# Stick keys' first eight k-tiles as a ninth seven-product group, woven with the sparse gate's first chunk, and the first taps issued before the values

## The chip, the cores and the metric

One core of a Trainium2 chip runs the whole kernel. The metric is the device time of one execution in microseconds; lower is better. Five engines work side by side, each through its own list of instructions: PE (TensorE, matmuls into PSUM), DVE (VectorE), ACT (ScalarE), POOL (GpSimd, which here issues DMAs) and SP (SyncE, which issues DMAs).

## What is computed

The reference is a decoder trunk of two layers over 256 tokens of 2048 features, in float32. Each layer projects its normalised input with one wide matrix and feeds three token mixers. Cut to what the change touches:

```python
h = rms_norm(x, norm_w)
proj = h @ w_in
(qa, ka, va, za, qi, ki, wi, ub, zb, qc, kc, vc, zc, gates) = jnp.split(proj, split_points(), axis=-1)
y_a = (dsa_attention(qa, ka, va, qi, ki, wi, top_k) * jax.nn.silu(za)) @ w_a_out
y_b = (conformer_conv(ub, conv_w, conv_b, cln_w, cln_b) * jax.nn.silu(zb)) @ w_b_out
kc = kc.reshape(b, s, C_HEADS, HEAD_DIM)
y_c = (stick_breaking_attention(qc, kc, vc) * jax.nn.silu(zc)) @ w_c_out
x = x + merged @ w_out
```

`kc` (1024 columns) are the keys of the stick-breaking attention, "stick keys" below. `za` (1024 columns) is the gate of the sparse attention. `conformer_conv` holds a causal depthwise convolution of 31 taps over 1024 channels.

## The kernel before, in words

**Units.** Weights arrive in units of two k-tiles by 512 columns (512 KB), by SP's queue into one of five `raw` buffers (`load_unit` L228, `raw_unit` L418). Float32 accuracy comes from splitting: ACT rounds the unit into `wh` (`high`, L255), DVE subtracts that from it into `wl` (`low`, L259), and PE forms three of the four products of high and low parts (`mult`, L270): 12 matmuls of 128x512 for 256 tokens. `wh` and `wl` have three buffers each, so the rounding of a unit waits until PE is through with the unit three before it. A chunk is 512 output columns: eight units, summed in two PSUM banks (`acc`, four banks in all; `mm` tiles, two of two banks each, serve for the rest).

**Leaving the banks.** `chunk_F` (L331) ends in `turned` (L308): DVE transposes the two banks into `zt` (L299, one buffer), POOL writes `zt` to DRAM (L302) and reads it back as `zy` (L308), and ACT or DVE then use it. The banks are free after DVE's transposes.

**Seven-product groups.** Class `Seven` (L459) does the first eight k-tiles of two chunks at once by a Strassen-like scheme: 14 half units of six matmuls in place of eight units of 12. The price is sums of weights on DVE (L511, L512, L524: 128x1024 each), some sums made by the DMA itself (`accum_op`, issued by POOL at L517 and L528), and a copy and a difference of banks (L573, L579). A group holds four `acc` banks (X, Y, Z, W). Eight such groups run per layer. The weights that are read twice lie in `ar` and in `ph` and `pl`. `gather` and `run` interleave a group's half units with plain units ("weave"), whose banks are then a two-bank `mm` tile (`wide_accs`).

**The taps.** The convolution is summed in one tile (`cv`) by `taps`: a tap is four `tap` instructions on DVE (L731, 128x256 each), or four products on ACT (L726) into a spare tile and one addition on DVE (L1032, 128x1024). `drain` (L205), called behind a unit's subtraction, issues the next piece; `pace` says of which kind ("2": two DVE taps, "s": products into `one`, of which there is one buffer, and their addition at the next call), `hold` stops it. A product group into `one` can start only when the addition of the group before it has read `one`.

**Order of a layer.** `values(0)`, `index_chunk(0)` and `index_chunk(4)` (each eight units, which share a bank of low-part products: ten matmul times per unit rather than 12), the convolution's input group `u` woven with the indexer's key steps, two more index chunks, the sparse keys and queries, the stick queries (two chunks), the stick keys (two chunks), the sparse gate (two chunks), `values(1)`, and so on. The sparse attention's three jobs (`attend`, L1297) run in the background of the stick queries, the stick keys and the gate; each of them goes through POOL's round trip once, and its last matmuls (L1355) wait for that. The scheduler keeps each engine's instructions in the order in which they were written, but for some that are marked as high in priority.

Of the kernel before, what the change touches and what calls it, by code (L numbers as in the profile page):

```python
# [14 lines left out]
P = 128  # L15
S = 256
NT = S // P
D = 2048
KD = D // P
CW = 1024  # L20
KC = CW // P
DEPTH = 2
NH = 8
# [7 lines left out]
LATER = 10  # L31
# [8 lines left out]
O_QA, O_KA, O_VA, O_ZA = 0, 1024, 1280, 1536  # L40
O_QI, O_KI, O_WI = 2560, 4608, 4736
O_UA, O_UG, O_ZB = 4752, 5776, 6800
O_QC, O_KC, O_VC, O_ZC, O_G = 7824, 8848, 9872, 10896, 11920
# [8 lines left out]
def trunk(ctx: ExitStack, tc: tile.TileContext, x, w_in, xt, w_a, w_b, w_c, w_out,  # L52
# [51 lines left out]
    def slot(dt=F32):  # L104
        return sp.tile([P, KC, S], dt, tag="s8", bufs=13, name=nm("s8"))
# [7 lines left out]
    def parts(n):  # L113
        return [slot(F32R).rearrange("p (k w) t -> p k w t", w=2) for _ in range(n // 4)]

    class Lazy(list):
        def __init__(self, n, make):
            super().__init__([None] * n)
            self.make = make
# [33 lines left out]
    waiting = []  # L153
# [11 lines left out]
    @contextmanager  # L165
    def in_turn():
        with tc.high_priority(offset=URGENT), issue_after(newest_parts[1].ins):
            yield
# [34 lines left out]
    hold, calls, pace, urgent = [False], [0], ["2"], [False]  # L203
# [106 lines left out]
    def turned(srcs, use, later=LATER, tmp=None, soon=False):  # L310


        n = len(srcs)
        if tmp is None:
            tmp = tp.tile([P, n * 512], F32, tag="zt", bufs=1, name=nm("zt"))
        c = srcs[0].shape[1]
        z = away([v.rearrange("p (k e) -> p k e", e=P) for v in srcs], tmp[:, :n * c], soon)

        def rest():
            y = tp.tile([P, n * 512], F32, tag="zy", bufs=1, name=nm("zy"))  # L320
            y = y[:, :n * c].rearrange("p (u k i) -> p u k i", u=n * 4, i=32)
            back(z, y)
            yield later - 2
            yield from use(y)

        pending.append([count[0] + 2, rest()])
# [7 lines left out]
    def chunk_F(w, c0, act, nk, use, later=LATER):  # L334
        turned(chunk_N(w, [(c0, 512)], act, nk), use, later)
# [81 lines left out]
    ring, spare = [0], [0]  # L417
# [24 lines left out]
    def once(make):  # L442
        kept = []

        def get():
            if not kept:
                kept.append(make())
            return kept[0]

        return get  # L450
# [8 lines left out]
    class Seven:  # L459


        def __init__(self, w, cols, act, sums, lead=7, own=None, adds=False):
            self.banks = banks = {}
            self.steps = {}

# [8 lines left out]
                return source(w, k * 4 + h * 2, 2, cols[n])  # L474

            area = [ar[:, h * 1024:(h + 1) * 1024].rearrange("p (k c) -> p k c", k=2) for h in range(2)]
            homes = area if own is None else {}
            third = {}

            def after_raw():  # L480
                return issue_after(last_raw[0].ins) if last_raw[0] is not None else nullcontext()

            def two(h):
                if own is not None:
                    homes[h] = own()[:, h * 1024:(h + 1) * 1024].rearrange("p (k c) -> p k c", k=2)
                with after_raw():
                    nc.sync.dma_start(homes[h], block(0, 1, h))

            def three(h):
                g = ("ph", "pl")[h]  # L490
                if own is not None:
                    third[h] = area[h]
                else:
                    third[h] = tp.tile([P, 1024], F32, tag=g, bufs=1, name=nm(g)).rearrange("p (k c) -> p k c", k=2)
                with after_raw():
                    nc.sync.dma_start(third[h], block(1, 1, h))
# [219 lines left out]
    def gate(c0, o, b, w, hx, done=None, attended=None):  # L716
        for k in range(0, KC, 4):
            chunk_F(w, c0 + k * P, hx, KD, partial(gate_use, k, o, b, (lambda k=k: done.count(k // 4) < NT) if done is not None else None, alone=done is attended),
                    LATER + 2 if k else LATER - 1)
# [47 lines left out]
    for layer in range(DEPTH):  # L767
# [255 lines left out]
        def taps(j, yT=yT, cv=cv, pr=pr, one=one, two=two, halves=halves):  # L1023

            o = cv[:, j * 4:j * 4 + 4, :]
            o2 = o.rearrange("p (t c) f -> p t (c f)", t=NT)
            state = dict(q=1, c=0, sum=None)

            def added():
                if state["sum"] is None:  # L1030
                    return False
                nc.vector.tensor_add(o2, o2, state["sum"])  # L1032
                state["sum"] = None
                return True

            halves.append(added)

            def begin():
                products_of(yT, pr, j, 0, o2, True)

            def go():
                by = pace[0][calls[0]]
                if added() and by == "s":
                    by = ""
                q = state["q"]
                if q < TAPS and by:
                    if state["c"] or by == "2":
                        for c in range(2):
                            tap(yT, cv, pr, j * 4 + state["c"] + c, q)
                        state["c"] = (state["c"] + 2) % 4  # L1050
                    else:
                        state["sum"] = one if by == "s" else two[:, q % 2]
                        products_of(yT, pr, j, q, state["sum"])
                    state["q"] += not state["c"]
                if state["q"] < TAPS or state["sum"] is not None:
                    waiting.insert(0, [0, [go]])

            waiting.append([4, [begin]])
            waiting.append([1, [go]])

        def use_u(j, y, yT=yT):
# [111 lines left out]
        def index_chunk(h):  # L1173
            acc, low_ = token_accs(), low_tile()
            for k0 in range(0, KD, 2):
                if (h, k0) in between:
                    between[h, k0]()
                background(index_unit(acc, low_, k0, unit(w, k0, 2, [(O_QI + h * P, 512)])))
            index_done(h, acc, low_)
# [8 lines left out]
        def values(j):  # L1188
            a = chunk_N(w, [(O_VC + j * 512, 512)], hx, KD, accs=None if j else wide_accs())
            if j:  # L1190
                with in_turn():
                    for f in halves:
                        f()
            for t in range(NT):
                with tc.high_priority():
                    nc.scalar.copy(vcr[:, t, j * 512:(j + 1) * 512], a[t])

        values(0)
        index_chunk(0)
        index_chunk(4)  # L1200
        def turn_first():
            with in_turn():
                turned(sgs, partial(use_u, 0))

        keys = key_steps()
        keys[7].at(0, turn_first)
        ring[0], spare[0] = 0, 10 ** 9
        run(gather("y*2 g.M1a y g.M5a g.M1b y g.M5b y g.M6a y g.M6b y g.M2a y g.M2b g.M7a g.M7b g.M3a c g.M3b c g.M4a d g.M4b c d c d d",
                   g=u, y=keys, c=ug, d=ua))
# [152 lines left out]
        for job in ((1, (0,)), (0, (0, 1)), (1, (1,))):  # L1362
            start(attend(*job))
        chunk_F(w, O_QC + 4 * P, hx, KD, partial(use_q, 4))
        pace[0] = "s2"

        kcT = slot()

# [1 line left out]
            nc.scalar.copy(blocks(kcT[:, h:h + 4, :]), by_feature(y))  # L1370
            yield 0

        for h in range(0, NH, 4):
            chunk_F(w, O_KC + h * P, hx, KD, partial(use_k, h))
        pace[0] = "s2"
        ga = parts(KC)
        gate(O_ZA, qaT, ga, w, hx, attended, attended)
        values(1)
        finish()
        settle()  # L1380
# [481 lines left out]
```

## Time and profile before

| what | value |
|---|---|
| median of 3 runs | 1982.86 us (1982.69 to 1982.94) |
| the profiled execution | 1982.91 us |
| its span in the trace | 1981.1 us |
| PE busy | 1970.6 us, 99% of the span |
| DVE busy | 1724.0 us, 87% |
| ACT busy | 1302.1 us, 66% |
| granted clock of TensorE | 0.999 of full speed |

PE is busy nearly all the time; its matmuls are pipelined, so a busy time says that matmuls followed each other, not how fast. The two layers have the same stages; the second runs some 983 us after the first. Times below are from the span's start.

### The profile page before, as it was taken

Reading aid. Unit: us, or ns where it says so; the run is one execution under the profiler, and the core shown is the slowest. Engines: PE = TensorE matmul, PEld = TensorE weight load, DVE = VectorE, ACT = ScalarE, POOL = GpSimd, SP = SyncE. Lnnn points to the kernel's source line nnn. Section 1 sums busy time; section 2 is a strip of 40 time slices with the busy share of each in tenths; the row PEclk is TensorE's granted clock in tenths of the full one; section 3 lists DMA queues with packets and bytes.
Section 4 is the critical chain, followed back from the end, with each engine's and each line's share of the span. In section 5 each row is a group of like instructions: output and inputs, shape, how many; then the busy total and the mean of one; then the engine's idle time right before and its main releaser. Section 6 shows DMA issues by size and latency. Waiting matters only on the chain. (4 is left out here: it accounts for less than half of the span.)

```text
span 1981.1 us, 26165 instructions
## 1 busy us (share of the span) xinstructions
PE 1970.6 (99%) x9194; PEld 1648.1 (83%) x9194; DVE 1724.0 (87%) x2054; ACT 1302.1 (66%) x1668; POOL 215.0 (11%) x320
## 2 busy tenths in 40 slices
PE   9999999999999999999999999999999999999998
PEld 8888888888888888888888888888888888888886
DVE  8798999989988979878786989999888888798786
ACT  7567666579875666564565666565898766565654
POOL 0021111200200001011100210121001000010010
PEclk9999999999999999999999999999999999999999
DMA  8888768876878778787978887688669688787894
GB/s 277 278 262 261 239 180 262 257 223 188 260 239 264 212 228 271 243 273 271 321 232 277 252 264 224 192 259 273 200 188 279 213 276 250 217 276 235 288 287 137
DMA packets 247557, 486.90 MB, mean 246 GB/s; under 512 B 17984, under 2 KB 30784, under 8 KB 247296
## 3 DMA queue, kind: packets, MB, share of 16 engines
q1 hardware_dynamic: 217472, 406.03, 63.2%
q0 software_dynamic: 28288, 76.04, 14.6%
q10 hardware_dynamic: 1664, 3.15, 0.4%
q8 instruction: 72, 1.18, 0.2%
q14 instruction: 61, 0.50, 0.1%
HBM read 452.38 MB, written 32.77 MB: 245 GB/s over the span
## 5 line engine op out<-in xcount | busy, mean ns | idle before, releaser
L270 PE MATMUL acc<-wh,s 128*128 128x512 f32 x4096 | 1039.8, 390 | 0.0
L255 ACT CAST wh<-raw 128x1024 fp32r<-128x1024 f32 (+1 forms) x639 | 666.9, 1046 | 416.6 <-PE acc L270 271.2
L259 DVE TENSOR_TENSOR wl<-raw,wh 128x1024 fp32r<-128x1024 f32 (+1 forms) x640 | 773.3, 1213 | 154.7 <-ACT wh L255 147.0
L270 PEld LDWEIGHTS acc<-wh,s 128*128 128x128 f32 x4096 | 761.4, 188 | 153.2 <-DVE acc L579 0.5
L270 PE MATMUL acc<-wl,s 128*128 128x512 f32 x1856 | 517.0, 390 | 0.0
L270 PEld LDWEIGHTS acc<-wl,s 128*128 128x128 f32 x1856 | 346.0, 188 | 74.8 <-DVE wl L259 4.4
L270 PE MATMUL mm<-wh,s 128*128 128x512 f32 (+1 forms) x1376 | 335.2, 385 | 0.0
L270 PEld LDWEIGHTS mm<-wh,s 128*128 128x128 f32 x1376 | 257.3, 188 | 50.9 <-ACT ev L1688 0.5
L302 POOL DMA_DIRECT2D z<-zt x192 | 113.2, 612 | 795.6 <-DVE zt L299 743.4
L270 PE MATMUL mm<-wl,s 128*128 128x512 f32 (+1 forms) x688 | 180.9, 385 | 0.0
L255 ACT CAST wh<-ar 128x1024 fp32r<-128x1024 f32 x92 | 96.9, 1053 | 81.0 <-PE acc L270 33.6
L270 PEld LDWEIGHTS mm<-wl,s 128*128 128x128 f32 x688 | 128.7, 188 | 24.4
L259 DVE TENSOR_TENSOR wl<-ar,wh 128x1024 fp32r<-128x1024 f32 x92 | 112.1, 1220 | 21.1 <-ACT wh L255 21.1
L731 DVE SCALAR_TENSOR_TENSOR s<-yT,cst,s 128x256 f32<-128x256 f32 x216 | 94.5, 476 | 0.1
L726 ACT ACTIVATE ar<-yT,cst 128x256 f32<-128x256 f32 x192 | 83.7, 499 | 15.4 <-DVE t L1330 12.6
L255 ACT CAST wh<-va 128x1024 fp32r<-128x1024 f32 x55 | 57.7, 1050 | 44.8 <-PE acc L270 19.5
L259 DVE TENSOR_TENSOR wl<-va,wh 128x1024 fp32r<-128x1024 f32 x55 | 67.1, 1219 | 20.6 <-ACT wh L255 20.6
L528 POOL DMA_DIRECT2D ar<-in_w_in_dram x28 | 33.8, 1220 | 453.0 <-DVE wl L259 453.0
L270 PEld LDWEIGHTS mm<-s,wl 128*128 128x128 f32 x512 | 66.9, 191 | 5.0
L308 POOL DMA_DIRECT2D zy<-z x50 | 36.1, 722 | 293.2 <-DMA z<-zt 75.8
L270 PE MATMUL mm<-s,wl 128*128 128x192 f32 x512 | 66.0, 271 | 0.0
L726 ACT ACTIVATE s<-yT,cst 128x256 f32<-128x256 f32 x88 | 40.4, 517 | 38.3 <-DVE s L1032 38.1
(284 smaller groups left out, 1463.3 us busy)
## 6 DMA issues: line engine op xcount, KB each, us to landing
raw<-in_w_in_dram SPq DMA_DIRECT2D x500, 512.0 KB, 4.6
raw<-in_w_out_dram SPq DMA_DIRECT2D x50, 512.0 KB, 5.5
zy<-z POOLq DMA_DIRECT2D x48, 512.0 KB, 5.8
z<-zt POOLq DMA_DIRECT2D x184, 128.0 KB, 5.0
ar<-in_w_in_dram SPq DMA_DIRECT2D x28, 512.0 KB, 6.3
ar<-in_w_in_dram POOLq DMA_DIRECT2D x28, 512.0 KB, 9.6
raw<-in_w_b_dram SPq DMA_DIRECT2D x26, 512.0 KB, 5.1
raw<-in_w_a_dram SPq DMA_DIRECT2D x24, 512.0 KB, 6.2
```

Source lines behind the costliest of these rows:

```text
L255: newest_parts[0] = nc.scalar.copy(u[1], u[0])
L259: newest_parts[1] = sub = nc.vector.tensor_sub(u[2], u[0], u[1].bitcast(F32))
L270: newest[0] = nc.tensor.matmul(o, lhsT, rhs, start=start, stop=stop, skip_group_check=True)
L302: nc.gpsimd.dma_start(z[:, :, :, a, :].rearrange("t b c e -> c (t b) e"), tmp[a * 32:(a + 1) * 32].rearrange("c t b k i -> c (t b) (k i)"))
L308: nc.gpsimd.dma_start(y.rearrange("p (t a) k i -> p t (a k i)", a=4), z.rearrange("t b c a e -> (b c) t (a e)"))
L528: nc.gpsimd.dma_start((homes if own is None else third)[h], block(1, 0, h), accum_op=ALU.add)
L726: nc.scalar.activation(v, yT[:, c, q:q + S], AF.Identity if bias else AF.Copy, scale=wq, **b)
L731: nc.vector.scalar_tensor_tensor(o, yT[:, c, q:q + S], wq, o, op0=ALU.mult, op1=ALU.add)
```

## The change

The change has three parts.

1. `Seven` takes `room`, two makers of slots in which the twice-read weights lie, in place of `ar`, `ph` and `pl`.
2. The stick keys' first eight k-tiles become such a group (`kg`). Its 14 half units are woven with the eight plain units of the gate's first chunk, which sum in a two-bank `mm` tile; the keys' last eight k-tiles (4 and 4 plain units, `kc_` and `kd_`) follow in the four `acc` banks; then comes the gate's second chunk as before. The keys' two chunks are turned at their last units with delays of 8 and 10 units.
3. The turn that gives the first half of the convolution's input stands ahead of `values(0)`, and the taps may run during `values(0)` and the two index chunks, at pace "s"; afterwards they are held until `u` as before. Pace "s2" around the stick queries and keys becomes "s".

```diff
--- before.py
+++ after.py
@@ -459,7 +459,7 @@
     class Seven:
 
 
-        def __init__(self, w, cols, act, sums, lead=7, own=None, adds=False):
+        def __init__(self, w, cols, act, sums, lead=7, own=None, adds=False, room=None):
             self.banks = banks = {}
             self.steps = {}
 
@@ -474,21 +474,23 @@
                 return source(w, k * 4 + h * 2, 2, cols[n])
 
             area = [ar[:, h * 1024:(h + 1) * 1024].rearrange("p (k c) -> p k c", k=2) for h in range(2)]
-            homes = area if own is None else {}
+            homes = area if own is None and room is None else {}
             third = {}
 
             def after_raw():
                 return issue_after(last_raw[0].ins) if last_raw[0] is not None else nullcontext()
 
             def two(h):
-                if own is not None:
-                    homes[h] = own()[:, h * 1024:(h + 1) * 1024].rearrange("p (k c) -> p k c", k=2)
+                if own is not None or room is not None:
+                    homes[h] = (own() if room is None else room[0]())[:, h * 1024:(h + 1) * 1024].rearrange("p (k c) -> p k c", k=2)
                 with after_raw():
                     nc.sync.dma_start(homes[h], block(0, 1, h))
 
             def three(h):
                 g = ("ph", "pl")[h]
-                if own is not None:
+                if room is not None:
+                    third[h] = room[1]()[:, h * 1024:(h + 1) * 1024].rearrange("p (k c) -> p k c", k=2)
+                elif own is not None:
                     third[h] = area[h]
                 else:
                     third[h] = tp.tile([P, 1024], F32, tag=g, bufs=1, name=nm(g)).rearrange("p (k c) -> p k c", k=2)
@@ -1055,7 +1057,7 @@
                 if state["q"] < TAPS or state["sum"] is not None:
                     waiting.insert(0, [0, [go]])
 
-            waiting.append([4, [begin]])
+            waiting.append([4 if j else 0, [begin]])
             waiting.append([1, [go]])
 
         def use_u(j, y, yT=yT):
@@ -1195,15 +1197,13 @@
                 with tc.high_priority():
                     nc.scalar.copy(vcr[:, t, j * 512:(j + 1) * 512], a[t])
 
+        turned(sgs, partial(use_u, 0), LATER - 2)
         values(0)
+        hold[0], pace[0] = False, "s"
         index_chunk(0)
         index_chunk(4)
-        def turn_first():
-            with in_turn():
-                turned(sgs, partial(use_u, 0))
-
+        hold[0], pace[0] = True, "2"
         keys = key_steps()
-        keys[7].at(0, turn_first)
         ring[0], spare[0] = 0, 10 ** 9
         run(gather("y*2 g.M1a y g.M5a g.M1b y g.M5b y g.M6a y g.M6b y g.M2a y g.M2b g.M7a g.M7b g.M3a c g.M3b c g.M4a d g.M4b c d c d d",
                    g=u, y=keys, c=ug, d=ua))
@@ -1362,7 +1362,7 @@
         for job in ((1, (0,)), (0, (0, 1)), (1, (1,))):
             start(attend(*job))
         chunk_F(w, O_QC + 4 * P, hx, KD, partial(use_q, 4))
-        pace[0] = "s2"
+        pace[0] = "s"
 
         kcT = slot()
 
@@ -1370,11 +1370,22 @@
             nc.scalar.copy(blocks(kcT[:, h:h + 4, :]), by_feature(y))
             yield 0
 
-        for h in range(0, NH, 4):
-            chunk_F(w, O_KC + h * P, hx, KD, partial(use_k, h))
-        pace[0] = "s2"
-        ga = parts(KC)
-        gate(O_ZA, qaT, ga, w, hx, attended, attended)
+        ga = Lazy(KC // 4, lambda: parts(4)[0])
+        room = [once(lambda: slot().rearrange("p a b -> p (a b)")) for _ in range(2)]
+        kg = Seven(w, (O_KC, O_KC + 512), hx, sums, 7, None, 3, room)
+        kc_, kd_ = ([plain(w, k0, O_KC + i * 512, hx, lambda v=v: [kg.bank(n) for n in v], False, k0 == KD - 2)
+                     for k0 in range(KC, KD, 2)] for i, v in enumerate(("XY", "ZW")))
+        for i, (v, st) in enumerate(zip(("XY", "ZW"), (kc_, kd_))):
+            st[-1].at(1, lambda i=i, v=v: turned([kg.bank(n) for n in v], partial(use_k, i * 4), LATER - 2 + 2 * i))
+
+        def gate_za(k):
+            return partial(gate_use, k, qaT, ga, lambda: attended.count(k // 4) < NT, alone=True)
+
+        za = chunk_steps(w, O_ZA, hx, KD, lambda a: turned(a, gate_za(0), LATER - 1), wide_accs)
+        ring[0], spare[0] = 0, 10 ** 9
+        run(gather("y*2 g.M1a y g.M5a g.M1b y g.M5b y g.M6a g.M6b y g.M2a g.M2b g.M7a y g.M7b y g.M4a c g.M4b c*3 g.M3a d g.M3b d*3",
+                   g=kg, y=za, c=kc_, d=kd_))
+        chunk_F(w, O_ZA + 4 * P, hx, KD, gate_za(4), LATER + 2)
         values(1)
         finish()
         settle()
```

Three places show how the instructions move. Numbers behind a name tell one buffer's use from the next; `raw`, `wh`, `wl` are a unit's weights and its two parts, `s8_82` is `one`, `s8_81` is `cv`, lines after the change stand two to eleven higher.

**ACT, from the first index chunk into the second.** Before:

```order
L255 CAST wh_133_804<-raw_132_802 128x1024
L255 CAST wh_136_824<-raw_135_822 128x1024
L255 CAST wh_139_844<-raw_138_842 128x1024
L255 CAST wh_142_864<-raw_141_862 128x1024
L255 CAST wh_151_897<-raw_150_895 128x1024
L255 CAST wh_154_917<-raw_153_915 128x1024
L255 CAST wh_160_945<-raw_159_943 128x1024
```

and now:

```order
L255 CAST wh_136_828<-raw_135_826 128x1024
L667 CAST s8_8_94<-t4_134_815 128x2x256
L728 ACTIVATE s8_82_540<-yT_80_537,cst_75 128x256 x4
L255 CAST wh_139_849<-raw_138_847 128x1024
L728 ACTIVATE s8_82_540<-yT_80_537,cst_75 128x256 x4
L255 CAST wh_142_873<-raw_141_871 128x1024
L255 CAST wh_145_894<-raw_144_892 128x1024
L728 ACTIVATE s8_82_540<-yT_80_537,cst_75 128x256 x4
L255 CAST wh_154_931<-raw_153_929 128x1024
L255 CAST wh_157_952<-raw_156_950 128x1024
L728 ACTIVATE s8_82_540<-yT_80_537,cst_75 128x256 x4
```

Between the roundings of units stand four products (L728) for every two units, into the one tile `s8_82`.

**DVE, second index chunk.** Before:

```order
L259 TENSOR_TENSOR wl_161_946<-raw_159_943,wh_160_945 128x1024
L259 TENSOR_TENSOR wl_164_966<-raw_162_963,wh_163_965 128x1024
L259 TENSOR_TENSOR wl_167_986<-raw_165_983,wh_166_985 128x1024
L259 TENSOR_TENSOR wl_170_1006<-raw_168_1003,wh_169_1005 128x1024
L259 TENSOR_TENSOR wl_173_1026<-raw_171_1023,wh_172_1025 128x1024
L259 TENSOR_TENSOR wl_176_1046<-raw_174_1043,wh_175_1045 128x1024
```

and now:

```order
L259 TENSOR_TENSOR wl_164_985<-raw_162_982,wh_163_984 128x1024
L1034 TENSOR_TENSOR s8_81_539<-s8_81_539,s8_82_540 128x1024
L259 TENSOR_TENSOR wl_167_1006<-raw_165_1003,wh_166_1005 128x1024
L259 TENSOR_TENSOR wl_170_1030<-raw_168_1027,wh_169_1029 128x1024
L1034 TENSOR_TENSOR s8_81_539<-s8_81_539,s8_82_540 128x1024
L259 TENSOR_TENSOR wl_173_1051<-raw_171_1048,wh_172_1050 128x1024
```

Behind the subtraction of every other unit stands the addition (L1034) which the next products on ACT wait for, and which itself waits for the products before.

**PE and DVE, where the gate's second chunk begins.** Before, PE goes from the gate's first chunk to its second, in `acc` banks that the stick keys had left a chunk earlier:

```order
L270 MATMUL acc_585_3390<-wl_617_3570,s8_5_91 128x512 x2
L270 MATMUL acc_586_3391<-wl_617_3570,s8_5_91 128x512 x2
L270 MATMUL acc_620_3595<-wh_623_3599,s8_2_88 128x512 x2
L270 MATMUL acc_621_3596<-wh_623_3599,s8_2_88 128x512 x2
L270 MATMUL acc_620_3595<-wh_623_3599,s8_2_88 128x512 x2
L270 MATMUL acc_621_3596<-wh_623_3599,s8_2_88 128x512 x2
```

Now PE comes from the keys' last plain unit, in the group's banks Z and W (`acc_566`, `acc_543`):

```order
L270 MATMUL acc_566_3276<-wh_619_3575,s8_5_91 128x512 x2
L270 MATMUL acc_543_3154<-wh_619_3575,s8_5_91 128x512 x2
L270 MATMUL acc_566_3276<-wl_620_3576,s8_5_91 128x512 x2
L270 MATMUL acc_543_3154<-wl_620_3576,s8_5_91 128x512 x2
L270 MATMUL acc_626_3637<-wh_629_3641,s8_2_88 128x512 x3
L270 MATMUL acc_627_3638<-wh_629_3641,s8_2_88 128x512 x2
```

and DVE has there:

```order
L668 TENSOR_TENSOR s8_362_2165<-s8_363_2168,s8_362_2165 128x512
L259 TENSOR_TENSOR wl_630_3642<-raw_628_3639,wh_629_3641 128x1024
L1034 TENSOR_TENSOR s8_81_539<-s8_81_539,s8_82_540 128x1024
L259 TENSOR_TENSOR wl_636_3676<-raw_634_3673,wh_635_3675 128x1024
L259 TENSOR_TENSOR wl_643_3722<-raw_641_3719,wh_642_3721 128x1024
L299 STREAM_TRANSPOSE zt_613_3536<-acc_534_3110 128x4x4x32
L299 STREAM_TRANSPOSE zt_613_3536<-acc_547_3173 128x4x4x32
```

`acc_534` and `acc_547` are the group's banks X and Y. PE's first matmuls into `acc_626` and `acc_627` wait for the two transposes (L299) out of these banks, and the transposes stand behind the subtraction into `wl_643`, which takes the buffer that PE reads as `wl_620`.

## Rows read from the trace of the kernel before

**Rows 1.** The page: span and busy time by engine.
```profile
span 1981.1 us, 26165 instructions
...
PE 1970.6 (99%) x9194; PEld 1648.1 (83%) x9194; DVE 1724.0 (87%) x2054; ACT 1302.1 (66%) x1668; POOL 215.0 (11%) x320
```

**Rows 2.** Busy time by stretch, first layer (us; DMA share and GB/s last).
```profile
core 0: us, PE busy (x) PEld busy (x) DVE busy (x) ACT busy (x) POOL busy (x), PEclk, DMA share, GB/s
89.10:107.30 18.20, 18.20 (x115) 16.23 (x115) 10.90 (x11) 8.77 (x10) 3.22 (x5) 1.00 1.00 339
309.80:356.50 46.70, 46.70 (x215) 38.96 (x214) 46.15 (x71) 29.62 (x53) 11.43 (x19) 1.00 0.85 262
```

**Rows 3.** What TensorE's weight loads waited for: total us, times, longest us.
```profile
PEld acc L270 <- DVE wl L259: 4.4, 20, 0.4
```

**Rows 4.** Timeline, 240 to 246 us: start, us, engine, line, tiles, count, idle before.
```profile
240.31 1.22 DVE L1032 TENSOR_TENSOR s<-s,s 128x1024 f32<-128x1024 f32 x1
240.42 1.98 PE L270 MATMUL acc<-wh,s 128*128 128x512 f32 x8
...
241.56 1.31 ACT L726 ACTIVATE s<-yT,cst 128x256 f32<-128x256 f32 x3 [0.75 <-DVE s L1032]
...
242.24 1.07 PE L270 MATMUL acc<-wl,s 128*128 128x512 f32 x4
...
242.78 1.03 ACT L255 CAST wh<-raw 128x1024 fp32r<-128x1024 f32 x1
...
243.84 1.23 DVE L259 TENSOR_TENSOR wl<-raw,wh 128x1024 fp32r<-128x1024 f32 x1 [0.24 <-ACT wh L255]
```

**Rows 5.** Timeline of ScalarE, 99 to 108 us.
```profile
99.80 1.05 ACT L255 CAST wh<-raw 128x1024 fp32r<-128x1024 f32 x1 [1.22 <-PE acc L270]
...
106.60 1.05 ACT L255 CAST wh<-raw 128x1024 fp32r<-128x1024 f32 x1 [1.41 <-PE acc L270]
107.56 0.80 ACT L1140 COPY t<-mm 128x768 f32<-128x768 f32 x1
```

**Rows 6.** Timeline of VectorE, 102 to 119 us.
```profile
103.00 0.99 DVE L259 TENSOR_TENSOR wl<-raw,wh 128x800 fp32r<-128x800 f32 x1 [0.89 <-ACT wh L255]
105.26 0.99 DVE L259 TENSOR_TENSOR wl<-raw,wh 128x800 fp32r<-128x800 f32 x1 [1.27 <-ACT wh L255]
106.17 1.22 DVE L511 TENSOR_TENSOR ph<-ph,ar 128x1024 f32<-128x1024 f32 x1
107.31 0.71 DVE L299 STREAM_TRANSPOSE zt<-acc 128x512 f32<-128x512 f32 x1
107.94 1.18 DVE L512 TENSOR_TENSOR ar<-ar,raw 128x1024 f32<-128x1024 f32 x1
...
112.23 1.23 DVE L259 TENSOR_TENSOR wl<-ar,wh 128x1024 fp32r<-128x1024 f32 x1 [0.47 <-ACT wh L255]
...
116.78 1.22 DVE L259 TENSOR_TENSOR wl<-raw,wh 128x1024 fp32r<-128x1024 f32 x1
```

**Rows 7.** Timeline of TensorE, 106 to 119 us.
```profile
106.40 1.03 PE L270 MATMUL mm<-s,wl 128*128 128x192 f32 x8
107.27 1.62 PE L270 MATMUL mm<-wh,s 128*128 128x400 f32 x8
...
118.05 0.73 PE L270 MATMUL acc<-wl,s 128*128 128x512 f32 x2
```

**Rows 8.** Timeline of VectorE, 336 to 339 us.
```profile
336.31 1.19 DVE L1330 SCALAR_TENSOR_TENSOR t<-mm,ar 128x1024 f32<-128x1024 f32 x1
...
337.80 1.21 DVE L1333 TENSOR_REDUCE sm<-t 128x8 f32<-128x1024 f32 x1
```

**Rows 9.** The page's groups: products that wait; and landing times (KB, us).
```profile
L726 ACT ACTIVATE s<-yT,cst 128x256 f32<-128x256 f32 x88 | 40.4, 517 | 38.3 <-DVE s L1032 38.1
...
zy<-z POOLq DMA_DIRECT2D x48, 512.0 KB, 5.8
z<-zt POOLq DMA_DIRECT2D x184, 128.0 KB, 5.0
```

## The prediction

> **What bounds the kernel now.** I read the page first: PE is busy for 1970.6 of 1981.1 us [rows 1], so only two things move the time, matmuls and gaps between them. The waits of PE's weight loads come next: the subtractions into `wl`, on which every unit hangs, delay PE 20 times by 0.4 us at most, 4.4 us in all [rows 3]. So DVE and ACT are just fast enough everywhere, and I look for where the change spends their lead. The table by stretch shows PE without a gap in the second index chunk and in the stick keys, at 1.00 of the granted clock, though the DMA engines are busy for all of the first stretch (339 GB/s) and DVE for 46.15 of 46.70 us of the second [rows 2]. The timelines then give durations and leads. A matmul of 128x512 starts every (242.24 - 240.42)/8 = 0.2275 us [rows 4].
>
> **The saving.** Eight units of 12 matmuls become 14 half units of six: 96 - 84 = 12 fewer per layer, 24 x 0.2275 = 5.5 us, all on PE's path. The Trainium skill ("TensorE: Matmul & The Clock Gate", Back-to-back issue gap) gives N/2.4 + 2.5 ns, about 216 ns for 512 columns; by that estimate the saving would be 5.2 us, and the rows, at 227, decide. Taps moved from DVE to ACT save nothing by themselves, since PE is the bound.
>
> **A, the index chunks.** In the second chunk PE takes 18.2/8 = 2.28 us a unit, 4.55 for two [rows 2]. There ACT now has four products into the one tile for every two units, and a ring of waits closes. The addition must end before the next products start (240.31 + 1.22 = 241.53, start 241.56), three products take 1.22 us up to the rounding behind them, so four take 1.63; the rounding takes 1.03 to 1.05, the subtraction follows 0.03 later (243.84) [rows 4]; the next operation on DVE comes 1.14 us behind such an operation (106.17 to 107.31 [rows 6]), and it is the addition: 1.63 + 1.05 + 0.03 + 1.14 + 1.22 + 0.03 = 5.10 us. That products wait for additions is seen before too: 88 of them waited 38.1 us in all [rows 9]. So ACT and DVE, each with idle time, together fall 0.55 us behind PE with every two units. Five such rings run from the end of the first chunk to the start of `u`: 2.75 us. What lead is there to spend? The unit rounded at 99.80 is ready at 100.85 [rows 5]; PE's low part of it starts at 106.40 [rows 7] and the six high matmuls before it 6 x 0.2275 = 1.37 us earlier, so the lead is 4.2 us. The first chunk spends it: over three units (6.8 us of PE) ACT has 11 products (4.5 us), three roundings at 0.96 (106.60 to 107.56 [rows 5]), four roundings of rotary queries (about 0.5 each, as I take from their half size), and a wait of about 0.8 for an addition that stands behind a subtraction: 10.2 us, 3.4 to 4 too many. I take 0.2 us of lead as left: **2.5 us**, between 1.0 (1.7 of lead left) and 3.5 (the first turn lands late and the rings start later, with no lead at all).
>
> **B, the start of `u`.** DVE there works from 103.00 to 116.78 + 1.22 = 118.00, less the idle 1.27 and 0.47: 13.3 us for six subtractions, five sums and two transposes [rows 6]. PE enters at 107.27 and needs the last of them at 118.05 [rows 7]: 10.8 us. It just fits, because DVE starts 4.27 us ahead. Behind the rings it starts when PE does: 13.3 - 10.8 = **2.5 us**. The lower end is 1.0, if A leaves lead, the upper end 2.7.
>
> **C, the start of the new group.** No trace has it; its list on DVE has the same operations. From the last plain unit's subtraction before it to the second M1 half's: nine operations at 1.14 (subtractions, sums, one addition of taps), two transposes at 0.63 (107.31 to 107.94 [rows 6]), L1330 and L1333 of the background attention at 1.10 and 1.13 (durations 1.19 and 1.21 [rows 8], of which some 0.09 lie under the next, as with the others) and the last at 1.22: 15.0 us. PE has 35 matmuls meanwhile, 8.0 us. Of the 7.0 us too many, a full lead covers 4.3 (a subtraction ends 1.25 us behind the rounding, at 102.1, and PE needs it at 106.40 [rows 5, 7]), somewhat more with units of 2.73 us; I take 5: **2.0 us**, between 1.0 and 2.7.
>
> **D, the bank.** The gate's second chunk begins right behind the keys' last unit, and all four `acc` banks belong to the group. Bank X is free after its transpose, which stands on DVE behind the subtraction of a unit that needs the buffers of that last unit. From the start of that unit's last high matmul: it ends after 1.07 - 3 x 0.2275 = 0.39 us [rows 4], then rounding 1.05, subtraction 1.14 to the next, transpose 0.71 [rows 6], with three hand-overs of 0.03: 3.38 us. PE has five matmuls there, 1.14 us. It waits **2.25 us**. The second transpose comes 0.63 later, under three matmuls. At best 2.0; at worst 4.3, if `zt` isn't free: the gate's first turn is written out by POOL in turns with the attention's, and such a write takes 5.0 us to land [rows 9]. Queued behind the transposes are only taps and subtractions that PE's own gap covers.
>
> **E, the attention's last job.** Its matmuls wait for a round trip through POOL whose eight writes are now mixed with the gate's, then a read of 5.8 us [rows 9], and they stand at a fixed place in PE's list. Between 0 and 2.8 us; I take 0.8, nearer to nothing because PE itself is late by then.
>
> **Costed at nothing:** the group's eight more loads and sums by DMA (covered as long as landings stay near those of the second index chunk, where PE had no gap at 339 GB/s [rows 2]), the fork and copies (fewer taps on DVE make room).
>
> **The sum** per layer: 2.5 + 2.5 + 2.0 + 2.25 + 0.8 = 10.05 lost, 2.73 won, 7.3 net; two layers 14.6. The profiled execution took 1982.91 us, 0.05 above the median and 1.8 above its span: 1982.9 + 14.6 = **1997.5 us**. Its own range, from the terms' ends (5.0 to 16.0 lost), is 1987.4 to 2009.4, and mostly 1991 to 2005.
>
> **The rivals.**
> - *The lead holds.* If the rings begin with their full lead, A and B nearly vanish: 5.05 - 2.73 = 2.3 per layer, **1987.5**. For it: ACT idles 1.22 us per unit before [rows 5]. Against: the ring is a chain of waits, and idle time on either engine doesn't shorten it.
> - *Only the bank waits* (C covered by lead as well, E nothing): 2 x (2.25 - 2.73) = -1.0, **1981.9**, no change.
> - *The other side, faster:* the transposes are the deciding point. If DVE gets to them before PE is through with the keys, D vanishes too and the saving stands: **1977.4**. That needs `wl_643` not to wait for the last unit; its buffer says that it does.
> - *Late transfers.* The group reads about 2 MB more per layer in the 93 us of keys and gate, against 262 GB/s now, some 23 GB/s more [rows 2]. If the twice-read weights or raw units land 2.5 us too late at the two tightest places, it adds 5 us per layer: **2007.5**.
> - *The clock falls.* Every stretch shows 1.00 granted [rows 2], with gaps of 0.4 us on the subtractions [rows 3]; the new ones are five times as long. At 1.2 in place of 2.4 GHz a matmul would take 0.455 us, and one stretch like the 10.8 us of B, once per layer, would cost 21.6: **2019**. The Trainium skill ("TensorE: Matmul & The Clock Gate", HAM oscillation — how this bites in real kernels) tells of kernels whose clock goes down between bursts; no run here shows it.
>
> **How the numbers follow.** The forecast has 0.56, late transfers 0.15, the holding lead 0.14, only the bank 0.06, the full saving 0.06, the clock 0.03. About 0.2% (4 us) is what a measurement can tell from no change: slower 0.88, same 0.06, faster 0.06. The range leaves out the last three cases and a part of the tails: 1985 to 2010.
>
> **What would show it.** In the profile after: PE's waits on `wh` (rounding) of about 0.55 us in a row between 88 and 112 us, then two on `wl` of some 1.2 us up to 125 us; one of 2 us on `wl` near 325; one on a transpose `zt` of 2.25 us near 380; all again in the second layer; 24 fewer matmuls. If PE's gaps on roundings in the index chunks are missing, A and B are wrong; if no gap on `zt` stands behind the keys, D is; a granted clock under 1.00 would show the last rival.

## The result and the profile after

The changed kernel takes 2009.47 us in the median of four runs (2006.23 to 2012.75) against 1982.78 before (four runs, 1982.64 to 1982.94): a ratio of 1.0135, 95% interval 1.0117 to 1.0152. It is slower, by 26.7 us where 14.6 were forecast; the forecast range of 1985 to 2010 holds it, barely. The profiled execution is the fastest of the four, at 2006.23, which is 23.3 over the profiled execution of before. The page of the changed kernel, against [rows 1]:

```profile
span 2004.2 us, 26277 instructions
...
PE 1974.8 (99%) x9170; PEld 1646.1 (82%) x9170; DVE 1736.0 (87%) x1980; ACT 1367.6 (68%) x1820; POOL 219.9 (11%) x324
```

24 matmuls fewer, yet the span is 23.1 us longer. What TensorE's weight loads waited for (us in all, times, longest us), against 4.4, 20 and 0.4 in [rows 3]:

```profile
PEld acc L270 <- DVE wl L259: 15.7, 21, 2.5
PEld acc L270 <- ACT wh L255: 7.6, 15, 0.7
```

and of the same kernel what the matmuls themselves waited for:

```profile
PE acc L270 <- DVE zt L299: 4.4, 2, 2.2
```

The subtractions (`wl`) now delay up to 2.5 us at once, the roundings (`wh`) 15 times up to 0.7, and two matmuls wait for a transpose (`zt`), one per layer. The timeline of TensorE shows where in the first layer (start, us, what, count, idle before and what ended it):

```profile
89.06 1.03 PE L270 MATMUL mm<-s,wl 128*128 128x192 f32 x8
90.41 1.65 PE L270 MATMUL acc<-wh,s 128*128 128x512 f32 x6 [0.33 <-ACT wh L255]
...
115.20 1.08 PE L270 MATMUL acc<-wh,s 128*128 128x512 f32 x4
117.29 0.73 PE L270 MATMUL acc<-wl,s 128*128 128x512 f32 x2 [1.01 <-DVE wl L259]
...
321.05 1.07 PE L270 MATMUL mm<-wl,s 128*128 128x512 f32 x4
321.96 1.07 PE L270 MATMUL acc<-wh,s 128*128 128x512 f32 x4
324.18 0.73 PE L270 MATMUL acc<-wl,s 128*128 128x512 f32 x2 [1.15 <-DVE wl L259]
...
329.77 0.84 PE L270 MATMUL mm<-wh,s 128*128 128x512 f32 x3
332.71 0.73 PE L270 MATMUL acc<-wl,s 128*128 128x512 f32 x2 [2.10 <-DVE wl L259]
...
385.25 1.07 PE L270 MATMUL acc<-wl,s 128*128 128x512 f32 x4
388.53 1.39 PE L270 MATMUL acc<-wh,s 128*128 128x512 f32 x5 [2.21 <-DVE zt L299]
...
390.04 1.48 PE L270 MATMUL acc<-wh,s 128*128 128x512 f32 x3
391.32 1.05 PE L270 MATMUL acc<-wl,s 128*128 128x512 f32 x2
```

A gap is best read from start to start, as ends are modelled: a row's start, less the start of the row above, less its matmuls at 0.2275 us. So behind 385.25 PE loses 388.53 - 385.25 - 4 x 0.2275 = 2.37 us (D), behind 321.96 and 329.77 it loses 1.31 and 2.26 (C), behind 115.20 1.18 (B). At 90.41 eight matmuls of 192 columns, which start every 0.109 us, leave 0.48 (A); this one comes back every 5.1 us. From 390.04 three matmuls take 1.28 us rather than 0.68: the clock.

**The ring (A)** on ScalarE, second chunk, in the timeline of the changed kernel:

```profile
87.71 1.71 ACT L728 ACTIVATE s<-yT,cst 128x256 f32<-128x256 f32 x4 [1.53 <-DVE s L1034]
89.33 1.98 ACT L255 CAST wh<-raw 128x1024 fp32r<-128x1024 f32 x2
92.85 1.71 ACT L728 ACTIVATE s<-yT,cst 128x256 f32<-128x256 f32 x4 [1.54 <-DVE s L1034]
```

Four products, two roundings, and then 1.54 us in which ACT waits for the addition (L1034). VectorE beside it:

```profile
90.39 1.23 DVE L259 TENSOR_TENSOR wl<-raw,wh 128x1024 fp32r<-128x1024 f32 x1 [1.64 <-ACT wh L255]
91.54 1.22 DVE L1034 TENSOR_TENSOR s<-s,s 128x1024 f32<-128x1024 f32 x1
```

It waits 1.64 us for the rounding and adds right behind the subtraction. Neither engine is full, each waits for the other, and the products start every 92.85 - 87.71 = 5.14 us (5.10 by the prediction's chain) where PE needs 4.55. In the page's groups the products into `one` now wait for their additions 69.3 us in all, 38.1 before [rows 9], with 272 products in place of 88:

```profile
L728 ACT ACTIVATE s<-yT,cst 128x256 f32<-128x256 f32 x272 | 121.0, 505 | 69.5 <-DVE s L1034 69.3
```

**The group's start (C)** on VectorE:

```profile
316.62 1.22 DVE L259 TENSOR_TENSOR wl<-raw,wh 128x1024 fp32r<-128x1024 f32 x1 [1.64 <-ACT wh L255]
317.77 1.22 DVE L1034 TENSOR_TENSOR s<-s,s 128x1024 f32<-128x1024 f32 x1
...
331.44 2.35 DVE L259 TENSOR_TENSOR wl<-raw,wh 128x1024 fp32r<-128x1024 f32 x2
```

The ring still turns right ahead of the group (1.64 us idle, addition at 317.77), and from then on VectorE is never idle up to the subtractions at 331.44, the first of which releases PE at 332.71. What it brought along as lead is small: the subtraction of the last plain unit ahead of the group ends at 316.62 + 1.22 = 317.84, and PE's low part of that unit starts at 321.05, 3.2 us later.

**The bank (D)** on VectorE: subtraction behind a rounding that waited for the buffer, then both transposes, then PE at 388.53:

```profile
386.53 1.23 DVE L259 TENSOR_TENSOR wl<-raw,wh 128x1024 fp32r<-128x1024 f32 x1 [1.45 <-ACT wh L255]
387.68 1.31 DVE L299 STREAM_TRANSPOSE zt<-acc 128x512 f32<-128x512 f32 x2
```

**The clock**, by windows of the changed kernel (columns as in [rows 2]):

```profile
core 0: us, PE busy (x) PEld busy (x) DVE busy (x) ACT busy (x) POOL busy (x), PEclk, DMA share, GB/s
387.00:389.00 2.00, 0.47 (x2) 0.45 (x3) 2.00 (x4) 0.62 (x2) 0.00 (x0) 1.00 1.00 338
389.00:391.00 2.00, 2.00 (x8) 1.54 (x8) 2.00 (x3) 1.32 (x3) 1.72 (x3) 0.73 1.04 381
391.00:393.00 2.00, 2.00 (x6) 1.54 (x5) 0.29 (x1) 1.99 (x3) 0.62 (x2) 0.50 1.02 338
393.00:395.00 2.00, 2.00 (x9) 1.65 (x8) 0.41 (x1) 1.93 (x4) 0.00 (x0) 0.92 0.18 57
1329.00:1331.00 2.00, 2.00 (x6) 1.52 (x6) 2.00 (x3) 1.66 (x4) 0.00 (x0) 0.50 0.85 254
1380.00:1388.00 8.00, 5.79 (x26) 4.46 (x25) 5.98 (x7) 5.23 (x10) 2.33 (x4) 1.00 0.98 351
```

It is 1.00 in the gap, falls to 0.50, TensorE's lower level of 1.2 GHz, some 1.5 us after PE has begun again (the matmuls from 390.04), and is back by 395. In the second layer the same gap D (window 1380 to 1388) costs no clock, but the one of C does (1329 to 1331). Each of these two falls costs PE 1.4 us in matmuls that start late. The Trainium skill ("TensorE: Matmul & The Clock Gate", Part 1: The HAM clock gate) says that the number of matmuls at the lower clock, at a kernel's start, varies from run to run. Here runs of the changed kernel differ by 6.5 us and those of before by 0.3, but no run shows that the clock makes this spread: the slowest, 2012.75 us, has the same mean granted clock on record as the traced one, 0.997.

The gaps of 0.15 us and more behind the kernel's start, first and second layer, beside the terms of the prediction (one of 0.18 us in each layer, at 573 and 1568 us, is left out):

| term | forecast | layer 1 | layer 2 |
|---|---|---|---|
| A, index chunks | 2.5 | 2.88 | 3.25 |
| B, start of `u` | 2.5 | 2.14 | 2.13 |
| stick queries (294 to 298 us) | none | 0.77 | 0.36 |
| C, start of the new group | 2.0 | 3.57 | 3.71 |
| D, bank | 2.25 | 2.37 | 2.37 |
| E, attention's last job (437 and 1432 us) | 0.8 | 0.15 | 0.30 |
| clock (layer 1 behind D, 2 behind C) | none | 1.40 | 1.40 |
| sum | 10.05 | 13.28 | 13.52 |

26.80 less the saving of 5.5 is 21.3 of the 23.1 us. Before had 1.6 us of such gaps of its own, 1.25 of them at 1538 us, which are gone now; so some 3 us lie in smaller delays that were not told apart.

### The profile page after: what moved, and what is told of

Read it like the earlier page. It is cut to its first block, busy times and chain, and to the rows that moved or that the text cites. A ratio compares the mean times of both kernels' runs of the same rounds, so it can differ in the third digit from the quotient of the medians.

```text
span 2004.2 us, 26277 instructions
## 1 busy us (share of the span) xinstructions
PE 1974.8 (99%) x9170; PEld 1646.1 (82%) x9170; DVE 1736.0 (87%) x1980; ACT 1367.6 (68%) x1820; POOL 219.9 (11%) x324
## 4 chain that ended last, share of the span: by engine, by line
PE 88%; DVE 5%; ACT 4%; issue 2%; DMA 1%; DVEq 0%; POOL 0%; ACTq 0%; POOLq 0%
PE acc L270 60%; PE mm L270 25%; ACT s L728 2%; DVE wl L259 1%; ACT wh L255 1%; DVE s L1034 1%; PE mm L1265 1%; PE mm L1355 0%; DVE zt L299 0%; PE mm L1465 0%; DMA raw<-in_w_in_dram 0%; PE mm L1412 0%; DMA z<-zt 0%; DMA zy<-z 0%; DVE ar L1224 0%
## 5 line engine op out<-in xcount | busy, mean ns | idle before, releaser
L270 PE MATMUL acc<-wh,s 128*128 128x512 f32 x3952 | 1009.1, 391 | 8.6 <-DVE zt L299 4.4
L255 ACT CAST wh<-raw 128x1024 fp32r<-128x1024 f32 x635 | 660.8, 1045 | 315.3 <-PE acc L270 187.8
L270 PEld LDWEIGHTS acc<-wh,s 128*128 128x128 f32 x3952 | 734.4, 188 | 161.0 <-ACT wh L255 7.6
L270 PE MATMUL acc<-wl,s 128*128 128x512 f32 x1784 | 500.7, 390 | 10.3 <-DVE wl L259 10.3
L270 PE MATMUL mm<-wh,s 128*128 128x512 f32 (+1 forms) x1504 | 368.4, 386 | 0.3 <-ACT wh L255 0.3
L270 PEld LDWEIGHTS mm<-wh,s 128*128 128x128 f32 x1504 | 281.6, 188 | 56.5 <-ACT wh L255 0.7
L270 PE MATMUL mm<-wl,s 128*128 128x512 f32 (+1 forms) x752 | 198.8, 386 | 0.0
L728 ACT ACTIVATE s<-yT,cst 128x256 f32<-128x256 f32 x272 | 121.0, 505 | 69.5 <-DVE s L1034 69.3
L1034 DVE TENSOR_TENSOR s<-s,s 128x1024 f32<-128x1024 f32 x64 | 77.7, 1215 | 4.1 <-ACT s L728 3.7
L728 ACT ACTIVATE ar<-yT,cst 128x256 f32<-128x256 f32 x144 | 63.6, 510 | 9.4 <-DVE ar L1225 8.1
```

Of the source, the lines that this page charges most:

```text
L255: newest_parts[0] = nc.scalar.copy(u[1], u[0])
L270: newest[0] = nc.tensor.matmul(o, lhsT, rhs, start=start, stop=stop, skip_group_check=True)
L728: nc.scalar.activation(v, yT[:, c, q:q + S], AF.Identity if bias else AF.Copy, scale=wq, **b)
```

## The experiments

Before's median on the chips of the experiments was 1982.23 (first four) and 1982.69 (last four). Gaps are told as above, from start to start.

**1 and 2. The early taps alone, on ACT or on DVE.** The kernel before with the third part of the change only, first as it is, then with another pace:

```diff
+        turned(sgs, partial(use_u, 0), LATER - 2)
         values(0)
+        hold[0], pace[0] = False, "s"
         index_chunk(0)
         index_chunk(4)
-        def turn_first():
-            with in_turn():
-                turned(sgs, partial(use_u, 0))
-
+        hold[0], pace[0] = True, "2"
         keys = key_steps()
-        keys[7].at(0, turn_first)
```

Experiment 2 has `"2"` in place of `"s"`; both begin the first taps without the delay of four calls, as the changed kernel does.

> The kernel before with the early taps alone: the first turn ahead of the values, products on ACT (pace s) in the two index chunks; no ninth group, the stick keys, the gate and the later paces as before. Theory (the ring products, rounding, subtraction, addition through the one spare tile, and the lead it spends): PE waits for roundings of about 0.5 us six times from about 84 to 111 us and twice for subtractions, 1.2 and 1.0 us, up to 123 us, as in the changed kernel; together 5.0 us a layer, so 1982.8 + 10 = 1993 us. Rival (the ninth group's extra loads slow the transfers and these delay the units everywhere): nothing of the kind without the group, 1983 us.

> As the run with the early taps alone, but the early taps are of the other kind (pace 2: two multiply-adds on DVE behind each subtraction, no products on ACT, no addition), as many taps in the same two chunks. Theory (the ring): DVE has 1.14 + 2 x 0.4 = 1.94 us a unit against PE's 2.28, nothing waits across engines, so the lead stays and the waits are gone: 1983 us. Rival (taps in these chunks cost whatever their kind, because DVE and ACT are too full at the start of u): 1988 to 1993 us.

Measured: 1995.24 (ratio 1.0065, 1.0051 to 1.0079) and 1982.56 (1.0004, 0.9995 to 1.0013). With the ring, TensorE's weight loads wait on roundings as in the changed kernel:

```profile
PEld acc L270 <- ACT wh L255: 8.0, 15, 0.7
```

Its gaps are those of A, B and the stick queries (first layer: 5.51 us up to 123 us, 0.39 at 273, 0.77 at 296 to 299), with none on transposes, no new group and no fall of the clock. With the same taps on DVE (windows of experiment 2, columns as in [rows 2]) PE never stops in either stretch, though DVE is busy for 28.00 of 28.00 us:

```profile
84.00:112.00 28.00, 28.00 (x172) 25.14 (x171) 28.00 (x43) 13.53 (x15) 3.96 (x7) 1.00 0.99 346
114.00:125.00 11.00, 11.00 (x56) 9.95 (x55) 11.00 (x12) 7.13 (x9) 0.23 (x1) 1.00 0.65 184
```

So A, B and what follows at the stick queries are the ring, not DVE's load (nor ACT's, which stands idle for 1.54 us of each turn): about 13 us of the change's 27.

**3. The bank mended in the changed kernel**, with pace "s2" around the stick queries as before:

```diff
-        chunk_F(w, O_ZA + 4 * P, hx, KD, gate_za(4), LATER + 2)
+        turned(chunk_N(w, [(O_ZA + 4 * P, 512)], hx, KD, accs=wide_accs()), gate_za(4), LATER + 2)
-        pace[0] = "s"
+        pace[0] = "s2"
```

> The changed kernel with the gate's second chunk summed in a two-bank mm tile in place of two acc banks, and pace s2 in place of s around the stick queries and keys. Theory (bank): the wait of 2.4 us on the transposes near 386 and 1382 us is gone, and with it the short fall of the granted clock behind it, while the waits in the index chunks, at u and at the start of the group (9 us a layer) stay: 2006 less 5 to 10, so 1996 to 2001 us. Rival (the wait is not the bank but DVE being late): a wait of about the same length at the same place on a subtraction instead, 2006 us.

Measured: 2009.01 (2004.75 to 2013.03; 1.0142, 1.0126 to 1.0157). No gap on `zt` is left, so D is the bank. But the time did not move by more than its spread of 8 us: C stays at 3.80 us (0.87 and 2.93) with a fall of the clock in the second layer, A and B are 1.4 us larger in the first layer, and 1.46 us of new gaps stand at 554 to 557 us, and again in the second layer. My forecast of 1996 to 2001 missed, since nothing of that was in it. The run changes the bank and the pace together, so it gives no price of the bank alone: the gaps at 554 us come back in experiment 7, which shares pace and early ring, and not in 4 and 5. That C stays with pace "s2" says also that the pace around the stick queries isn't what makes it.

**4. Bank mended and early taps on DVE** (experiment 3 with experiment 2's pace).

> The changed kernel with all three: early taps on DVE (pace 2) in the index chunks, the gate's second chunk in an mm tile, pace s2 around the stick queries and keys. Theory (ring, lead and bank are the whole loss): waits in the index chunks, at u and on the transposes are gone; of those at the start of the group, which began with less lead, some 0.6 us a layer is left; the 24 matmuls saved then show: 1982.8 - 5.5 + 1.5 = 1979 us, and the granted clock is as in the kernel before. Rival (the group's loads and sums cost by themselves): 1984 us or more.

Measured: 1985.43 (1982.90 to 1990.53; 1.0019, 1.0010 to 1.0028). A, B, D and the gaps at 554 us are gone (0.56 us at 82 us is left of the first stretch), C is one gap of 2.70 us, in layer 2 0.57 and 2.96 with a fall of the clock behind it. Its cause is another one, on VectorE of this kernel:

```profile
312.41 1.23 DVE L513 TENSOR_TENSOR s<-s,s 128x1024 f32<-128x1024 f32 x1 [2.51 <-DMA s<-in_w_in_dram]
```

The first sum of the group (L513) waits 2.51 us for a load. The queue of SyncE shows why (start, us of the row, what, count):

```profile
293.63 10.99 SPq L425 DMA_DIRECT2D raw<-in_w_in_dram  x5
304.68 0.46 SPq L487 DMA_DIRECT2D s<-in_w_in_dram  x1
```

The loads of the twice-read weights (L487, L498) are issued from 304.68 on, behind five loads of plain units that had to wait for `raw` buffers since 293.63. That is the prediction's rival of late transfers, at one place and once PE is on time; in the changed kernel VectorE comes to this sum at 320.04, out of work that never pauses, and doesn't wait.

**5. The twice-read weights loaded a chunk earlier**: experiment 4 with the group made, and its four loads issued, ahead of the stick queries' second chunk.

```diff
+        kg = Seven(w, (O_KC, O_KC + 512), hx, sums, 0, None, 3, room)
+        for h in range(2):
+            kg.three(h)
+            kg.two(h)
         chunk_F(w, O_QC + 4 * P, hx, KD, partial(use_q, 4))
...
-        kg = Seven(w, (O_KC, O_KC + 512), hx, sums, 7, None, 3, room)
```

> As the run with both mended, and the new group's four loads of twice-read weights are issued during the stick queries' second chunk, ahead of that chunk's last raw units, in place of behind the first five raw units of the weave (where they landed at 312.4 us and DVE idled 2.5 us for them). Theory (late transfers at this one place): the gap of 2.7 to 3.0 us at the start of the group is gone in both layers, with the clock's fall behind it; what is left is the saving: 1982.3 - 5.5 + 0.5 = 1977.3 us, and the runs lie close together. Rival (the list of DVE there is too long whatever the loads do): a gap of 2 us or more stays, 1983 us.

Measured: 1979.34 (1977.51 to 1982.27; 0.9984, 0.9975 to 0.9993), 0.2% faster than the kernel before. On SyncE's queue the four loads now go out between 270 and 285 us:

```profile
270.48 0.46 SPq L498 DMA_DIRECT2D s<-in_w_in_dram  x1
...
284.18 0.54 SPq L487 DMA_DIRECT2D s<-in_w_in_dram  x1
```

C falls to 0.44 us in each layer and the clock stays at 1.00. VectorE comes to the group with more lead: its subtraction of the last plain unit, and PE's low part of it,

```profile
308.76 1.22 DVE L259 TENSOR_TENSOR wl<-raw,wh 128x1024 fp32r<-128x1024 f32 x1
```

```profile
316.41 1.07 PE L270 MATMUL mm<-wl,s 128*128 128x512 f32 x4
```

are 316.41 - 309.98 = 6.4 us apart, where the changed kernel has 3.2. Of the saving of 5.5 us 3.35 arrive in the median. The traced execution is the slowest of the eleven (1982.27); in it single gaps of 0.2 to 1.1 us take the rest.

**6, 7. One cause put back into that kernel**: the gate's second chunk into `acc` banks (6), the early taps at pace "s" (7).

> As the run with early loads, but the gate's second chunk sums in acc banks again, as in the changed kernel. Theory (bank): PE waits for a transpose zt behind the keys' last unit, 2.25 us if only the subtraction stands before it, up to 4 where zt's one buffer is late as well, and behind a gap of that length the clock may fall (some 1.7 us each time): 4.5 to 11 us more than the run with early loads, 1982 to 1988 us. Rival (with the lead kept, DVE is through with the transposes in time): the same as the run with early loads.

> As the run with early loads, but the early taps are products on ACT again (pace s in the two index chunks). Theory (ring and lead): waits of 0.5 us in the index chunks and of 1.2 and 1.0 at u come back, 5.0 to 5.5 us a layer; at the start of the group no lead stands against DVE's list and 2 us a layer are lost though the loads are early: 14 to 17 us more, 1992 to 1995 us. Rival (the gap at the group's start was the loads alone): 10 to 11 us more, 1988 us.

Measured for 6: 1996.07 (1.0068, 1.0054 to 1.0082), 16.7 us over experiment 5. Its gap on `zt` is 381.13 - 376.28 - 0.91 = 3.94 us, for here taps on DVE (L733) stand between the last subtraction and the transposes; then PE waits 2.54 us, at 385.71, on the attention's second job (its last, E, comes at 434 us), and from 381 to 390 us the granted clock is 0.50. Timeline of VectorE, then of TensorE:

```profile
377.95 1.22 DVE L259 TENSOR_TENSOR wl<-raw,wh 128x1024 fp32r<-128x1024 f32 x1
379.09 1.27 DVE L733 SCALAR_TENSOR_TENSOR s<-yT,cst,s 128x256 f32<-128x256 f32 x3
380.27 1.31 DVE L299 STREAM_TRANSPOSE zt<-acc 128x512 f32<-128x512 f32 x2
```

```profile
376.28 1.07 PE L270 MATMUL acc<-wl,s 128*128 128x512 f32 x4
381.13 2.05 PE L270 MATMUL acc<-wh,s 128*128 128x512 f32 x4 [3.78 <-DVE zt L299]
```

Measured for 7: 2006.07 (1.0120, 1.0105 to 1.0136), 26.7 us over experiment 5. A and B are back (5.48 us), and so is C, as one gap of 3.05 us with a fall of the clock, though the loads are early. VectorE ahead of the group, and PE's low part of the last plain unit:

```profile
314.57 1.22 DVE L1034 TENSOR_TENSOR s<-s,s 128x1024 f32<-128x1024 f32 x1
...
318.57 1.23 DVE L259 TENSOR_TENSOR wl<-raw,wh 128x1024 fp32r<-128x1024 f32 x1 [0.85 <-ACT wh L255]
```

```profile
323.03 1.07 PE L270 MATMUL mm<-wl,s 128*128 128x512 f32 x4
```

The lead is 323.03 - 319.80 = 3.2 us, against 6.4 in experiment 5. Additions right ahead of the group are not the difference, as experiment 5 has them too (at 301.06 and 307.10). The lead is short long before: at one unit of the stick queries it is 0.6 us (subtraction from 277.81, PE at 279.59), in experiment 5, at the same unit, 4.1 (268.84, 274.15). Where between the index chunks and there it is lost is not shown.

Both forecasts had the direction; the times came out 8 and 11 us beyond their upper ends. That for 6 had the gap at up to 4 us, as measured, and a fall of the clock at 1.7 us; but the clock stayed low for some 10 us (7 in the second layer), and the wait on the attention's second job was not in it. That for 7 had C at 2 us where it measured 3.05, and left out the falls of the clock (1.4 us a layer), the gaps at 556 to 559 us (1.46 a layer, as in experiment 3) and those of the stick queries.

C in the four kernels with a mended bank, first layer:

| C (us) | loads late | loads early |
|---|---|---|
| early taps as a ring | 3.80 (exp. 3) | 3.05 (exp. 7) |
| early taps on DVE | 2.70 (exp. 4) | 0.44 (exp. 5) |

Either cause alone costs most of it: the two delays run side by side, and taking away one uncovers the other.

**8. The changed kernel without early taps** (first taps behind `u` again).

> The changed kernel with the early taps undone alone (the first turn at the key steps' eighth unit, as in the kernel before); group, weave, bank and the later pace s as changed. Theory (the early taps pay for the additions that the group puts on DVE): the waits in the index chunks and at u are gone, 10 us, those at the group's start and on the bank stay, and the taps that are not done by then meet the work of the stick attention and of the last groups at 525 to 560 us, so that PE waits there for several us at a time: 2010 us or more. Rival (the early taps only cost): 2006 - 10 = 1996 us.

Measured: 2030.26 (one run), 20.8 us over the changed kernel. A and B are gone, 0.86 us is left where D was and C is 3.8, but the group's sums take DVE's time for taps; 56 products are left behind 500 us (14 in the changed kernel, by the windows of L728), and eleven of them come in a row. ScalarE there:

```profile
525.69 4.50 ACT L728 ACTIVATE ar<-yT,cst 128x256 f32<-128x256 f32 x11
531.83 1.04 ACT L255 CAST wh<-va 128x1024 fp32r<-128x1024 f32 x1 [1.64 <-DMA va<-in_w_a_dram]
532.78 2.10 ACT L728 ACTIVATE ar<-yT,cst 128x256 f32<-128x256 f32 x5
...
535.48 1.98 ACT L255 CAST wh<-raw 128x1024 fp32r<-128x1024 f32 x2
```

and TensorE beside it:

```profile
536.56 2.50 PE L270 MATMUL acc<-wh,s 128*128 128x512 f32 x5 [8.05 <-ACT wh L255]
```

PE waits 8.05 us for a rounding behind 11 products, 1.64 us for a load and 5 products more, and as long in the second layer. So the early taps are what pays for the ninth group here (2009.47 with them, 2030.26 without); by experiments 4 and 5 the engine chosen for them was the mistake.

## Why the prediction was right, and where it fell short

- **Sign and mechanism.** The matmuls fell by 24 and the time rose, as forecast, by gaps at A, B, C and D where they were said to be (C in two gaps). A and B together were sized at 5.0 and measured 5.0 and 5.4; experiments 1 and 2 show the ring behind both. D was sized at 2.25 and measured 2.37; experiment 3 shows the bank behind it.
- **C was mis-sized**: 2.0 forecast, 3.57 and 3.71 measured, above its own upper end of 2.7. The failing step is "I take 5" for the lead: it was read from the kernel before, while the changed kernel has 3.2 there (317.84 to 321.05), and 7.0 too many less 3.57 lost leaves 3.4. Experiments 5 and 7 show that the early ring takes it: 6.4 us without, 3.2 with it. The list of 15.0 us was good: from 317.77 to 331.44 + 1.22 it took 14.9.
- **The clock** was a rival of 0.03 with one price, a whole stretch at half speed. It did fall, behind some gaps of over 2 us, for 2 to 4 us each: 2.8 us in the traced run. The Trainium skill's case ("TensorE: Matmul & The Clock Gate", HAM oscillation — how this bites in real kernels), a clock that goes down between bursts, is not quite what happened: here it fell behind single gaps in a full stream, and behind two of the four of over 2 us. It belonged into the forecast as a small addition to each such gap.
- **Not in the sum**: the stick queries' 0.77 and 0.36, which come with the ring alone (experiment 1 has 0.77 too), and smaller delays of some 3 us, against which 1.6 us of before's own gaps are gone.
- **E** was 0.8 and is 0.15 and 0.30 here (437.66 - 436.60 - 0.91 in the first layer). In experiment 5, where PE comes to it some 6 us earlier, it is 0.81 us in the first layer, which agrees with "PE itself is late by then".
- **"Costed at nothing"** for the loads was right only because DVE came later than they did: with that mended C is 2.70 us through them (experiment 4), and 0.44 once they are early.
- In us over both layers: C +3.3, clock +2.8, A +1.1, stick queries +1.1, B and D -0.5, E -1.2, the rest +1.8; that is the 8.5 between 14.6 and the profiled 23.1. The 3.2 us from the profiled run to the median were not traced.
- **Luck.** The range ends 0.5 us above the median, and two of the four runs lie beyond it. It holds the median although the clock, the stick queries and the small delays were not in it, because its upper ends for D and E had room that was not needed.

## What to carry to other kernels

A temporary with one buffer that two engines pass back and forth is a ring: its period is the sum of both engines' work and hand-overs, and it can set the pace while either engine has idle time. Lead that one stage spends is missing in the next, so size a list of work by the lead of the changed kernel, not of the old one. Where several causes meet at one wait, mending one may give little (C: 3.80 to 3.05 or 2.70 us with one mended, 0.44 with both); put each back into the version with all of them mended to see its price.

## What was not expected of the hardware

The granted clock fell to 0.50 behind single gaps of 2.2 to 3.9 us and not behind each of them (1.00 throughout behind D in the second layer, and behind the 2.93 us of experiment 3 in the first), and came back within 2 to 4 us where PE kept on. Where waits went on at the lower clock, as in experiment 6, it stayed low for some 10 us, and the bank's gap of 3.94 us became, with the job's wait, 10.1 us of lost starts in that layer (6.8 in the second). DVE busy for all of 28 us, on the other hand, held PE up nowhere in that stretch (experiment 2).
